# Raw tiles of the second MLP matrix move into room of their own, and the first pair's final norm is due three steps later

## The chip, the cores and the metric

The kernel runs on one core of a Trainium2 chip. The metric is the device time of one execution in microseconds (us), taken as the median of several runs; lower is better. Profiled executions show where the time goes. The engines are TensorE (PE, with its weight loads as PEld), VectorE (DVE), ScalarE (ACT), GpSimd (POOL) and SyncE (SP), which does nothing here but issue transfers.

## The reference

One decoder layer on 2048 positions of width 1024, all in float32, and a final norm:

```python
h = rms_norm(x, norm1_g)
proj = einsum('bsd,dc->bsc', h, w_in)             # u_a, v_a, val_b, gate_b, 512 columns each
a_out = gelu(u_a) * (tril(w_s) @ layer_norm(gelu(v_a)) + b)      # in chunks of 128 positions
b_out = silu(group_layer_norm(conv31(val_b * sigmoid(gate_b))))  # causal, depthwise
x = x + einsum('bsc,cd->bsd', concat([a_out, b_out]), w_out)
h = rms_norm(x, norm2_g)
x = x + einsum('bsf,fd->bsd', relu(h @ w_ff1) ** 2, w_ff2)       # 1024 -> 4096 -> 1024
return rms_norm(x, final_g)
```

## The kernel before, in words

**Tiles.** The positions are four blocks (b = 0..3) of 512. Activations lie with features on the 128 partitions and positions along the free axis. Every product is done three times in a rounded float32 form, high by high, high by low and low by high (`mm3`, line 177), so each operand exists as a high part (a cast on ScalarE) and a low part (a subtraction, `rest`, line 161, on GpSimd or VectorE).

**Stages.** Input projections, gating and the depthwise convolution run block by block; the convolution is a chain of 31 VectorE operations over a tile `g` of gated values (`conv_chain`, line 263) with a tail of transposes and a norm (`conv_tail`). The lists `waiting`, `chains` and `tails` hold convolutions not begun, under way, and at their tails. `stage_o` is the output projection of one block. Then the MLP runs for pairs of blocks, pair 0 being blocks 0 and 1. Both MLP products are done by a seven-product scheme on 2 by 2 blocks: i = 1, 5, 6, 2, 7, 3, 4, where products 5, 6, 7, 3 (and on one side others) use sums or differences of blocks.

The order is: `stage_o(0)` and the rest of the front, `stage_o(1)`, the first up projection (`multiply("u0", ...)`), `stage_o(2)`, `stage_o(3)`, the second up projection (`multiply("u1", ...)`), then the down projection, eight pieces of pair 0 and eight of pair 1 (`down_chunk`, line 1175). One product of an up projection is 12 matmuls of 512 columns; an up projection has 112 of them, 16 units of 7. A piece of the down projection has 28 steps of 6 matmuls, in the order of `STEPS`, line 1073.

**The second matrix ahead of time.** `w_2` is prepared while the up projections run: its 16 matrices go through a pipe, `w2st` (line 901), of five stages: load the raw blocks, make the sum or difference, cast the high part, subtract the low part, store the operand to memory. The down projection reads the operands back. How fast the pipe goes is `pace["w2"]`, in steps per call of `beside`: `W2_PACE` has 0.3 in the first up projection, 0.2 in `stage_o(2)`, 0.65 in the second up projection, 0.7 in the down projection. One matrix is seven steps. The pipe's call is `w2st.run(k - 1, k, k + 1, k + 1, k + 2)`: stores up to k - 1, low parts up to k, high parts and sums up to k + 1, loads up to k + 2. The first matrix has a pipe of its own, `wst`, of the same kind. Both are filled by `left` (line 826): `loader` takes two tiles for a matrix, the first with the blocks `r11` and `r12`, the second with `r21` and `r22`, and issues two loads of 512 KB on SyncE; `maker` makes the sums. In the order 1, 5, 6, 2, 7, 3, 4 the first tile is last read when the difference of i = 3 (sixth) is made, the second by the low part of i = 4 (seventh). The last two tiles of each matrix are thus in use for most of its seven steps.

**Room.** `slots` is a pool of 41 tiles of 4 KB a partition. It serves raw tiles, operands, the 28 `hop` tiles (7 sums for each of 4 feature pairs) that an up projection reads, the residual, the down projection's inputs and operands. `gpool` has 7 tiles of 542 floats for `g`. `t2` and `wsum` hold smaller working tiles. A new tile takes a place whose last user is done; an instruction that writes it waits for that user. All queues are in order: a load that waits on SyncE holds up every later one there.

**Order.** Blocks under `tc.manual_schedule()` run in the order in which the code issues them: `stage_o(1)` to the end of the second up projection, and the very last piece. The other pieces of the down projection are ordered by a planner, by the code's order and by what it reckons to be ready.

**The final norm.** When the last sums of a block are added up in the last piece of its pair, `finish(b, acc)` (line 1118) is put into `queue`. Its squares are summed by GpSimd in `square_add`. `tick(n)` advances the first generator of the queue n times. In the down projection a step with j = 3 gives two advances, j = 0 and j = 2 one each, j = 1 none. `finish` lets `gaps[0]` advances pass, sums the squares over the features with narrow matmuls (`ssum`), then makes the reciprocal root, spreads it (`rbc`), and scales and stores eight tiles, one an advance. Block 1's `finish` starts at step (3, 3) of pair 0's last piece; block 0's follows it in the queue.

Of the kernel before, what the change touches and what calls it, by code (L numbers as in the profile page):

```python
# [9 lines left out]
F32 = mybir.dt.float32  # L10
# [5 lines left out]
P = 128  # L16
# [16 lines left out]
G_SLOTS = 7  # L33
T_SLOTS = 10
W_SUMS = 6
# [5 lines left out]
TAIL_STEPS = (3, 1, 2)  # L41
# [41 lines left out]
def hybrid_block_kernel(  # L83
# [26 lines left out]
    def pool(stack, name, bufs, psum=False):  # L110
        return stack.enter_context(tc.tile_pool(
            name=name, bufs=bufs, reuse_waits="tile",
            space=bass.MemoryType.PSUM if psum else bass.MemoryType.SB))

    slots = pool(ctx, "slots", SLOTS)
    gpool = pool(ctx, "gpool", G_SLOTS)
    t2 = pool(ctx, "t2", T_SLOTS)
    wsum = pool(ctx, "wsum", W_SUMS)
    banks = {}
    early = ctx.enter_context(ExitStack())  # L120
    banks["mm"] = pool(early, "ps_mm", MM_BANKS, True)
    banks["cv"] = pool(early, "ps_cv", 2, True)
# [8 lines left out]
    def slot(name, dtype=F32):  # L131
        return slots.tile([P, 1024], dtype, tag="s", name=name)
# [5 lines left out]
    def tmp(name, dtype=F32):  # L138
        return t2.tile([P, 512], dtype, tag="tmp", name=name)
# [4 lines left out]
    def mm_tile(name):  # L144
        return bank("mm", name)
# [4 lines left out]
    def tiny(name, n=4):  # L150
        return small.tile([P, n], F32, tag=f"{name}{n}", name=name)
# [92 lines left out]
    def v(off, j):  # L244
        return vec[:, off + j:off + j + 1]
# [15 lines left out]
    waiting, chains, tails = [], [], []  # L261
# [222 lines left out]
    def feature_sums(acc, n, pc=None):  # L484

        pc = tp_tile("ssum") if pc is None else pc
        for i in range(n):
            for k, sq in enumerate(acc):
                pe4.matmul(pc[:, i:i + 1], sq[:, i * P:(i + 1) * P], ones[:, 0:1],
                           start=k == 0, stop=k == len(acc) - 1)  # L490
        return pc[:, :n]
# [251 lines left out]
    late, _ = stage_v(1, h[1], parts[1])  # L743
# [4 lines left out]
    late, _ = stage_v(2, h[2], parts[2])  # L748
# [9 lines left out]
    late, _ = stage_v(3, h[3], parts[3])  # L758
# [64 lines left out]
    def order_of(units):  # L823
        return ORDER if len(units) == 1 else ORDER2

    def left(src, units, tag):

        raw, sums = {}, {}

        def loader(m):  # L830
            def load():
                raw[m] = [slot("wraw"), slot("wraw")]
                for a in range(2):
                    nc.sync.dma_start(raw[m][a], src[m, a])
            return load

        def maker(m, i):
            def make():
                (r11, r12), (r21, r22) = [(t[:, :512], t[:, 512:]) for t in raw[m]]
                if i in (5, 6):  # L840
                    sums[m, i] = wsum.tile([P, 512], F32, tag="ws", name="ws")
                out, x, y, op = {
                    5: (sums.get((m, 5)), r21, r22, ALU.add),
                    6: (sums.get((m, 6)), sums.get((m, 5)), r11, ALU.subtract),
                    7: (r21, *((r11, r21) if tag == "w2" else (r21, r11)), ALU.subtract),
                    3: (sums.get((m, 5)), r12, sums.get((m, 6)), ALU.subtract)}.get(i, [None] * 4)
                if out is None:
                    return {1: r11, 2: r12, 4: r22}[i]
                dsb.tensor_tensor(out, x, y, op=op)
                return out  # L850
            return make

        for i in order_of(units):
            for m in units:
                yield (tag, m, i), loader(m) if i == 1 else lambda: None, maker(m, i)
# [21 lines left out]
    def multiply(tag, groups, pair, out, at):  # L877
        bks, rhs, n = {}, hops[pair], 0
        for units in groups:
            for i in order_of(units):  # L880
                for m in units:
                    w = wst.get((tag, m, i))
                    out(m, i, product(i, m, bks, w, rhs[i]))
                    used[0] += 1
                    u = used[0]
                    lag = (3, 4, 5, 7) if n > 16 else (2, 3, 4, 6)
                    beat()
                    wst.run(u, *(min(u + k, 112 * (pair + 1)) for k in lag))
                    beside()
                    at(n)  # L890
                    n += 1
# [77 lines left out]
    def up_out(pair):  # L969
        kept = {}  # L970

        def out(m, i, ps):
            blk_ = INTO[i]
            def copy():
                kept[m, blk_] = tmp("c")
                nc.scalar.copy(kept[m, blk_], ps)

            def finish():
                if i == 4:
                    src, c = ps, tmp("c")  # L980
                else:
                    c = kept.pop((m, blk_))
                    src = c if i == 7 else ps
                    dve.tensor_tensor(src, ps, c, op=ALU.add)
                (dsb if i == 7 else dve).scalar_tensor_tensor(
                    c, src, 0.0, r_rows[:, blk_[1], :], op0=ALU.max, op1=ALU.mult)
                later(1, lambda: nc.scalar.activation(c, c, AF.Square))  # L987
                later(2, lambda: nc.scalar.dma_start(
                    f_d[pair][m // 2, 2 * blk_[0] + blk_[1], :, m % 2, :], c))

            later(1, copy if i in (1, 5, 6) else finish, True)
        return out

    def reopen_banks(old, phase, **count):
        old.close()
        st = ctx.enter_context(ExitStack())
        for kind, n in count.items():
            banks[kind] = pool(st, f"ps_{kind}_{phase}", n, True)
        return st
# [52 lines left out]
    with tc.manual_schedule():  # L1052
        stage_o(1, first_at(0))
        multiply("u0", UNITS, 0, up_out(0), at_up0)
    mid = early if waiting or chains or tails else reopen_banks(early, "m", mm=6, tp=2)
    with tc.manual_schedule():
        stage_o(2, at_o2)
        pace["w2"] = 0.0
# [58 lines left out]

    def finish(b, acc):

        gaps = (3, 3, 4) if b < 2 else TAIL_STEPS  # L1120
        for _ in range(gaps[0]):
            yield
        r = tiny("r1")
        ve = tiny("ve")
        ps = feature_sums(acc, 4, mm_tile("ssum"))
        yield
        dve.tensor_scalar(ve, ps, 1.0 / D, EPS, op0=ALU.mult, op1=ALU.add)
        gps.tensor_tensor(r, ve, nhalf.to_broadcast([P, 4]), op=ALU.pow)
        for _ in range(gaps[1]):
            yield  # L1130
        dg = tmp("dg")
        times_ident(dg, r)
        for _ in range(gaps[2]):
            yield
        ps = mm_tile("rbc3")
        pe4.matmul(ps, ones, dg, start=True, stop=True)
        x = dn["x"][b]
        for k in range(KD):
            yield
            dve.scalar_tensor_tensor(x[k], x[k], v(V_FG, k), ps, op0=ALU.mult, op1=ALU.mult)  # L1140
            nc.sync.dma_start(out[b, k // 2, :, k % 2, :], x[k])

    def times_ident(dg, r):
        dsb.tensor_tensor(
            dg.rearrange("p (n t) -> p n t", t=P), ident.unsqueeze(1).to_broadcast([P, 4, P]),
            r.unsqueeze(2).to_broadcast([P, 4, P]), op=ALU.mult)
# [28 lines left out]
    def down_chunk(pair, n, after):  # L1175
# [4 lines left out]
        for i, j in STEPS:  # L1180
            bank_, first = BANK[i]
            a, t = INTO[i]
            if first:
                bks[bank_, j] = mm_tile("py")
            ps = bks[bank_, j]
            for m in range(2):
                hl = [o[:, m * 512:m * 512 + 512] for o in ops[i]]
                mm3(ps, [w2[i][m][:, k, j * P:(j + 1) * P] for k in range(2)], hl,
                    first and m == 0, m == 1)
            x = dn["x"][2 * pair + t][2 * j + a]  # L1190
            dve.tensor_tensor(x, ps, x, op=ALU.add)
            if n == 7 and LAST[a, t] == i:
                done[t] += 1
                last = pair == 1 and t == 0
                square_add(accs[t], x, last and done[t] > 6)
                if done[t] == 8:
                    f = (finish_last if last else finish)(2 * pair + t, accs[t])
                    (ends if last else queue).append(f)
            if j == 3:
                after(n, i)  # L1200
                beside(2)
            elif j == 1:
                beside(0)
            else:
                tick(1)
# [88 lines left out]
```

## Time and profile before

| what | us |
|---|---|
| median of 3 runs | 1842.84 |
| lowest and highest run | 1842.77, 1843.34 |
| the profiled execution | 1846.86 |
| its span, first to last instruction | 1845.0 |

In the span the stages lie as follows, by TensorE's work in the timeline: input projections, gating and output projections of blocks 0 and 1 up to about 491 us, first up projection to 802 us, output projections of blocks 2 and 3 to 892 us, second up projection to 1198 us, down projection to 1830 us. The lines of the profile on which the argument rests stand in the prediction. In a line of groups or of the timeline, "[2.30 <-POOL sq L78]" means that the engine was idle for 2.30 us before this instruction and that an instruction of GpSimd writing a tile `sq` ended that. L78 is the line of a helper through which most operations are issued, so the tile's name tells more than the line.

### The profile page before, as it was taken

Reading aid. Unit: us, or ns where it says so; the run is one execution under the profiler, and the core shown is the slowest. Engines: PE = TensorE matmul, PEld = TensorE weight load, DVE = VectorE, ACT = ScalarE, POOL = GpSimd, SP = SyncE. Lnnn points to the kernel's source line nnn. Section 1 sums busy time; section 2 is a strip of 40 time slices with the busy share of each in tenths; the row PEclk is TensorE's granted clock in tenths of the full one; section 3 lists DMA queues with packets and bytes.
Section 4 is the critical chain, followed back from the end, with each engine's and each line's share of the span. In section 5 each row is a group of like instructions: output and inputs, shape, how many; then the busy total and the mean of one; then the engine's idle time right before and its main releaser. Section 6 shows DMA issues by size and latency. Waiting matters only on the chain.

```text
span 1845.0 us, 23225 instructions
## 1 busy us (share of the span) xinstructions
PE 1810.2 (98%) x8068; PEld 1492.0 (81%) x8068; DVE 1340.5 (73%) x1826; ACT 757.7 (41%) x1169; POOL 1232.4 (67%) x774
## 2 busy tenths in 40 slices
PE   9999989999999999999999999999999999999996
PEld 7888877888888888888887887888788878888885
DVE  5699997997899985632566686778766668665555
ACT  5345554554445455455454545433312131222112
POOL 4575984983766667699777988777855465444434
PEclk9999999999999999999999999999999999999998
DMA  8342654532545455685556878999987779767742
GB/s 323 112 165 93 222 177 180 204 131 82 209 151 196 162 193 201 216 294 197 205 187 227 294 251 292 355 399 375 374 336 259 256 248 333 294 240 259 263 162 91
DMA packets 131685, 424.72 MB, mean 230 GB/s; under 512 B 14576, under 2 KB 15216, under 8 KB 131568
## 3 DMA queue, kind: packets, MB, share of 16 engines
q1 hardware_dynamic: 96288, 329.64, 50.5%
q10 hardware_dynamic: 35280, 93.60, 13.0%
q8 instruction: 63, 1.03, 0.2%
q14 instruction: 54, 0.44, 0.1%
HBM read 302.60 MB, written 120.59 MB: 229 GB/s over the span
## 4 chain that ended last, share of the span: by engine, by line
PE 85%; DVE 7%; POOL 3%; DMA 2%; issue 2%; ACT 1%; SPq 0%; DVEq 0%; ACTq 0%; POOLq 0%
PE py L78 48%; PE pz L78 8%; PE po L78 8%; PE px L78 4%; PE pg L78 4%; PE pvv L78 4%; PE pu L78 4%; DVE acc L78 3%; PE pv L78 3%; DMA wraw<-in_w 1%; PE sgu L78 1%; DVE nb L78 1%; DVE ws L78 1%; PE rbc L78 1%; POOL sq L78 1%
## 5 line engine op out<-in xcount | busy, mean ns | idle before, releaser
L78 PE MATMUL py<-fo_hi,w2o 128*128 128x512 f32 x1792 | 555.6, 391 | 0.0
L78 POOL TENSOR_TENSOR fo_lo<-fraw,fo_hi 128x1024 fp32r<-128x1024 f32 x111 | 275.6, 2493 | 255.4 <-ACT fo_hi L158 219.9
L78 DVE TENSOR_TENSOR x<-py,x 128x512 f32<-128x512 f32 x448 | 299.8, 687 | 181.1 <-PE py L78 180.9
L78 PEld LDWEIGHTS py<-fo_hi,w2o 128*128 128x128 f32 x1792 | 337.3, 188 | 70.5 <-issue 0.5
L78 PE MATMUL py<-hop,w1o 128*128 128x512 f32 x1536 | 364.2, 391 | 4.0 <-ACT w1o L806 2.3
L78 PE MATMUL py<-fo_lo,w2o 128*128 128x512 f32 x896 | 350.1, 391 | 1.5 <-POOL fo_lo L78 1.4
L78 PEld LDWEIGHTS py<-hop,w1o 128*128 128x128 f32 x1536 | 287.5, 188 | 66.5 <-ACT w1o L806 3.1
L78 DVE SCALAR_TENSOR_TENSOR acc<-g,vec,acc 128x512 f32<-128x512 f32 x464 | 322.8, 746 | 1.2
L158 ACT CAST fo_hi<-fraw 128x1024 fp32r<-128x1024 f32 x112 | 116.9, 1052 | 408.2 <-PE py L78 218.6
L78 POOL TENSOR_TENSOR w_lo<-raw,w_hi 128x1024 fp32r<-128x1024 f32 (+1 forms) x94 | 224.2, 2392 | 56.0 <-ACT w_hi L158 39.0
L78 POOL TENSOR_TENSOR w1o<-wraw,w1o 128x512 fp32r<-128x512 f32 x120 | 172.0, 1437 | 58.6 <-ACT w1o L806 48.7
L78 PEld LDWEIGHTS py<-fo_lo,w2o 128*128 128x128 f32 x896 | 168.5, 188 | 38.6 <-POOL fo_lo L78 3.0
L78 PE MATMUL pz<-hop,w1o 128*128 128x512 f32 x768 | 183.8, 390 | 0.0
L78 POOL TENSOR_TENSOR w1o<-ws,w1o 128x512 fp32r<-128x512 f32 x90 | 128.7, 1433 | 67.4 <-ACT w1o L806 66.1
L78 PEld LDWEIGHTS pz<-hop,w1o 128*128 128x128 f32 x768 | 143.8, 188 | 29.7
L78 DVE TENSOR_TENSOR fraw<-fraw 128x1024 f32<-128x1024 f32 x64 | 94.9, 1483 | 13.9 <-POOL fo_lo L78 13.8
L78 PE MATMUL po<-m_hi,w_hi 128*128 128x512 f32 x256 | 101.2, 395 | 0.0
L78 PE MATMUL po<-m_hi,w_lo 128*128 128x512 f32 x256 | 99.9, 390 | 0.6 <-POOL w_lo L78 0.6
L987 ACT ACTIVATE c<-c 128x512 f32<-128x512 f32 x128 | 80.7, 631 | 48.0 <-DVE c L78 46.6
L78 PE MATMUL po<-m_lo,w_hi 128*128 128x512 f32 x256 | 99.7, 389 | 0.0
L78 POOL TENSOR_TENSOR w2p<-wraw,w2p 128x512 fp32r<-128x512 f32 x64 | 93.7, 1465 | 3.8 <-ACT w2p L806 3.8
L78 DVE TENSOR_TENSOR px<-px,c 128x512 f32<-128x512 f32 x32 | 22.4, 699 | 101.0 <-PE px L78 69.9
(150 smaller groups left out, 2956.7 us busy)
## 6 DMA issues: line engine op xcount, KB each, us to landing
w2o<-w_d SPq DMA_DIRECT2D x224, 512.0 KB, 6.2
w_d<-w2p ACTq DMA_DIRECT2D x112, 512.0 KB, 5.1
wraw<-in_w SPq DMA_DIRECT2D x92, 512.0 KB, 4.9
f_d<-c ACTq DMA_DIRECT2D x128, 256.0 KB, 4.1
fraw<-f_d SPq DMA_DIRECT2D x64, 512.0 KB, 6.9
raw<-in_w_ct SPq DMA_DIRECT2D x48, 512.0 KB, 5.2
raw<-in_w_o SPq DMA_DIRECT2D x32, 512.0 KB, 5.1
w1o<-w_d SPq DMA_DIRECT2D x28, 512.0 KB, 5.7
```

The lines of the kernel that those rows point to most:

```text
L78: return op(out, *args, **kwargs)
L158: nc.scalar.copy(hi, src)
L987: later(1, lambda: nc.scalar.activation(c, c, AF.Square))
```

## The change

The pool `gpool` is opened last among the working pools, in a stack of its own. When the first up projection is issued, `gpool` is closed and a pool of three 4 KB tiles, `more["w2"]`, is opened in its place. From then on the loader of `w_2` takes its two raw tiles from there instead of from `slots`; the loader of `w_1` has no entry in `more` and goes on with `slots`. The PSUM banks are reopened at that point without the condition that stood there. In `finish`, the first gap for blocks 0 and 1 is 6 advances instead of 3.

```diff
     slots = pool(ctx, "slots", SLOTS)
-    gpool = pool(ctx, "gpool", G_SLOTS)
-    t2 = pool(ctx, "t2", T_SLOTS)
-    wsum = pool(ctx, "wsum", W_SUMS)
-    banks = {}
+    sb = ctx.enter_context(ExitStack())
+    t2 = pool(sb, "t2", T_SLOTS)
+    wsum = pool(sb, "wsum", W_SUMS)
+    gst = sb.enter_context(ExitStack())
+    gpool = pool(gst, "gpool", G_SLOTS)
+    banks, more = {}, {}
...
             def load():
-                raw[m] = [slot("wraw"), slot("wraw")]
+                p = more.get(tag)
+                raw[m] = [slot("wraw") if p is None else p.tile(
+                    [P, 1024], F32, tag="m", name="wraw") for _ in range(2)]
                 for a in range(2):
                     nc.sync.dma_start(raw[m][a], src[m, a])
...
         multiply("u0", UNITS, 0, up_out(0), at_up0)
-    mid = early if waiting or chains or tails else reopen_banks(early, "m", mm=6, tp=2)
+    mid = reopen_banks(early, "m", mm=6, tp=2)
+    gst.close()
+    more["w2"] = pool(sb, "more", 3)
     with tc.manual_schedule():
         stage_o(2, at_o2)
...
-        gaps = (3, 3, 4) if b < 2 else TAIL_STEPS
+        gaps = (6, 3, 4) if b < 2 else TAIL_STEPS
         for _ in range(gaps[0]):
             yield
```

## The prediction, made before the change was run

> **What bounds the kernel now.** I read the page first, then the waits of TensorE from the last product of the first pass onward, then the stages as windows, then the waits of SyncE's queue, and last the timeline around each TensorE stop.
>
> ```profile
> span 1845.0 us, 23225 instructions
> PE 1810.2 (98%) x8068; PEld 1492.0 (81%) x8068; DVE 1340.5 (73%) x1826; ACT 757.7 (41%) x1169; POOL 1232.4 (67%) x774
> ```
>
> TensorE is busy 98% of the span, so 34.8 us is all that any change to waits could win, and most of that lies where this change cannot reach. The waits of TensorE from 800 us to 1560 us (who <- whom: us in total, times, longest) are what it can reach:
>
> ```profile
> PE py L78 <- ACT w1o L806: 2.3, 1, 2.3
> PE ssum L78 <- POOL sq L78: 2.3, 1, 2.3
> PE py L78 <- POOL fo_lo L78: 1.4, 2, 1.2
> PE py L78 <- ACT c L976: 1.4, 1, 1.4
> PE po L78 <- POOL w_lo L78: 0.6, 1, 0.6
> ```
>
> They sum to 8.0 us. The stages (us, then busy time and count for PE, PEld, DVE, ACT, POOL, then clock, DMA share, GB/s):
>
> ```profile
> 892.00:998.00 106.00, 106.00 (x470) 87.14 (x470) 69.27 (x73) 53.97 (x98) 78.11 (x56) 1.00 0.58 207
> 1109.00:1120.00 11.00, 9.62 (x42) 7.64 (x42) 4.15 (x6) 6.14 (x12) 7.63 (x6) 1.00 0.95 323
> 1180.00:1279.00 99.00, 99.00 (x439) 81.98 (x438) 78.64 (x88) 32.97 (x47) 71.67 (x38) 1.00 1.02 399
> ```
>
> Undisturbed, TensorE does 470 matmuls in 106 us, 0.226 us each. In the second up projection the DMA engines have room (0.58); from 1180 us they are full (1.02). Behind the first and fourth wait stands SyncE. Its own waits in the second up projection, 892 to 1170 us:
>
> ```profile
> SPq L834 <- PE py L78: 82.0, 13, 23.9
> SPq L834 <- DMA w_d<-w2p: 57.2, 12, 8.6
> SPq L834 <- DVE ws L78: 52.5, 6, 17.7
> SPq L834 <- POOL w1o L78: 25.1, 6, 7.6
> ```
>
> Line 834 loads raw weights, `w_1` and `w_2` alike. A load reads an input that nobody writes; what it waits for is a tile of `slots`: the product, the store, the difference or the remainder named is the last user of that tile. So SyncE stands at this line for most of the stage because the 41 tiles are all taken. They hold 28 `hop` tiles (7 sums by 4); 13 are left for raw tiles of two matrices, operands, and operands on their way to memory.
>
> **The change part by part.** First the room.
>
> ```profile
> L78 DVE SCALAR_TENSOR_TENSOR c<-g,vec,acc x16: 731/738/748, 114.5 to 682.1; 128x512 f32<-128x512 f32 x16
> L309 ACT ACTIVATE y<-cb,vec x8: 760/774/790, 420.0 to 711.0; 128x512 f32<-128x512 f32 x8
> ```
>
> The last tap reads a `g` tile at 682.1 us and the last tail ends by 712 us; the reopening stands behind the first up projection, whose last products run until 802 us. So the three lists in the condition on line 1055 are empty, the unconditional reopening does what was done before, and opening the new pool waits for nothing. The room suffices: seven tiles of 542 floats are 15,176 bytes a partition, three of 1024 floats are 12,288. No instruction is added or removed.
>
> What moves is which tile a `w_2` load gets. One matrix holds two raw tiles for seven steps; at 0.65 steps a product that is 10.8 products, 29 us, and the next pair is loaded before the first is free. So two to four of the 13 loose tiles come back to `w_1`, operands and stores. What that is worth is read at the two stops:
>
> ```profile
> 990.59 8.85 SPq L834 DMA_DIRECT2D wraw<-in_w  x4
> 996.90 1.73 POOL L78 TENSOR_TENSOR w2p<-wraw,w2p 128x512 fp32r<-128x512 f32 x1
> 1004.82 0.62 ACT L806 CAST w1o<-wraw 128x512 fp32r<-128x512 f32 x1 [4.01 <-DMA wraw<-in_w]
> 1007.42 0.62 ACT L806 CAST w1o<-ws 128x512 fp32r<-128x512 f32 x1 [1.45 <-DVE ws L78]
> 1008.08 2.08 PE L78 MATMUL py<-hop,w1o 128*128 128x512 f32 x8 [2.31 <-ACT w1o L806]
> ```
>
> Four loads take SyncE 8.85 us, where four issues of 0.33 us would take 1.3: the second pair stood until the remainder of a `w2p`, ending at 998.63 us, gave up its raw tile. That pair is `w_1`'s (its cast makes a `w1o`); it landed 4 us after ScalarE wanted it, and TensorE stopped 2.31 us. Issued some 7 us earlier it is in time: **-2.3 us**.
>
> ```profile
> 1107.47 1.37 DVE L78 TENSOR_TENSOR ws<-wraw,ws 128x512 f32<-128x512 f32 x1
> 1108.99 3.68 SPq L834 DMA_DIRECT2D wraw<-in_w  x4
> 1117.38 0.62 ACT L806 CAST w2p<-wraw 128x512 fp32r<-128x512 f32 x1 [3.74 <-POOL w1o L78]
> 1117.91 0.58 ACT L976 COPY c<-py 128x512 f32<-128x512 f32 x1
> 1118.54 3.02 PE L78 MATMUL py<-hop,w1o 128*128 128x512 f32 x12 [1.38 <-ACT c L976]
> ```
>
> Here two pairs leave together right after a difference freed a tile. ScalarE then stands 3.74 us before a cast of a raw `w_2` tile (the releaser named had ended before; I take it to be the load), the copy queued behind it clears the bank late, and TensorE stops 1.38 us. A first tile free beforehand lets the load go ahead: **-1.4 us**. Both bounds of these two terms: 0 if something else is late at once, -3.7 as taken. Below that nothing is to be had there, since no other stop stands in the stage.
>
> What is late next is what the three tiles cost. Pair m takes tiles A and B, pair m+1 C and A, so the second load of a pair waits until step 3 of the matrix before has made its difference (sixth of seven steps), one step (1.5 products, about 4.2 us) before the load's own place. Behind that wait stand all later loads on SyncE, `w_1`'s among them. The first operand needs tile C only, and tile A is first read three steps, some 12 us, after it came free. A load takes
>
> ```profile
> wraw<-in_w SPq DMA_DIRECT2D x42, 512.0 KB, 5.1
> w2o<-w_d SPq DMA_DIRECT2D x70, 512.0 KB, 8.7
> ```
>
> 5.1 us here (second row: 8.7 us for the operands' reloads once the engines are full, 1180 to 1360 us), so the cover is about 7 us, and I cost this wait at 0; without cover it is a rival below.
>
> The down projection has one stop of this kind, at its third piece:
>
> ```profile
> 1303.55 0.50 PE L78 MATMUL py<-fo_lo,w2o 128*128 128x512 f32 x1 [1.20 <-POOL fo_lo L78]
> 1170.60 3.03 SPq L1068 DMA_DIRECT2D x<-x_d  x3
> ```
>
> Transfers are full from 1180 us, so what starts earlier before then is a lead that lasts. The residual's eight reloads begin at 1170.60 us, behind the last waiting raw loads, while the engines have room; two or three tiles more start two or three of them earlier, at 1.3 us each (0.5 MB at 399 GB/s) a lead of 2.6 to 3.9 us against stops of 1.4 in sum. I take **-1.4 us**; its bounds are -1.4 and, if the order of the loads turns out worse, the same stop doubled, +1.4. The 0.6 us at `w_lo` stays: GpSimd runs
>
> ```profile
> 844.56 7.11 POOL L78 TENSOR_TENSOR w_lo<-raw,w_hi 128x1024 fp32r<-128x1024 f32 x3
> ```
>
> three in a row there, and no raw `w_2` tile is in its way.
>
> Now the norm three steps later. `finish(1)` is queued at step (3,3) of the pair's last piece; with a gap of 3 its sums come due after (2,2), step 23 of 28, with 6 after (4,0), step 25. But the stage up to there is ordered by the planner:
>
> ```profile
> 1197.00:1511.20 314.20, 304.48 (x1338) 250.85 (x1338) 1.00 0.86 324
> 1507.51 4.97 POOL L78 TENSOR_TENSOR sq<-sq 128x512 f32<-128x512 f32 x4
> 1511.30 1.05 PE L78 MATMUL ssum<-ones,sq 128*128 128x1 f32 x8 [2.30 <-POOL sq L78]
> 1512.44:1515.85 3.41, 3.41 (x9) 2.63 (x9) 0.81 (x2) 0.87 (x1) 3.34 (x3) 0.50 0.58 204
> 1522.51 5.34 DVE L78 SCALAR_TENSOR_TENSOR x<-x,vec,rbc 128x512 f32<-128x512 f32 x8
> ```
>
> The first row counts the matmuls with a `w2o` before the sums: 1338 = 7 x 168 + 162, so they stand after step 27, not 23. The last row shows why: eight scalings that the code spreads over eight ticks run back to back, so the planner places what it reckons ready. It reckoned the squares ready only at step 27; a due step of 25 is still earlier, and the place stays. The stop costs 2.3 us and then 3.41 us at half clock, where 9 matmuls ran instead of 15: 6 x 0.226 = 1.4. Bounds 0 and **-3.7**; I take 0, because the rule read off the rows gives it. The eight scalings and stores come later by some 3 us for one block and 6 for the other; they end long before the span does and cost nothing.
>
> The half clock follows a stop of 2.3 us plus eight matmuls one column wide, while the 2.31 us stop at 1008 us left the clock at 1.00. The Trainium skill, page "TensorE: Matmul & The Clock Gate", section "Why this matters for your kernels", asks for idle gaps over some 3 us before the rate drops; by it alone the norm's term would be 2.3. The trace has the drop after a shorter one, and decides.
>
> Sum against the profiled execution: -2.3 - 1.4 - 1.4 = **-5.1 us** of 1846.86 us (span 1845.0 us and 1.9 around it). That execution lies 4.0 us over the median of the runs, 1842.84 us; the stops are waits, so I carry the same -5.1 over: 1837.7 us.
>
> **The rivals.** (a) The norm's stop goes as well: the planner's place slips past the end of the piece, or slots shift GpSimd's order. For it: two steps are 12 x 0.226 = 2.7 us, more than the 2.3 missing. Against: the readiness above. -5.1 - 3.7 = -8.8: **1834.0**.
>
> (b) Transfers or ScalarE's order keep the stops: the load is not late for its tile but for the engines. For it: DMA share 0.95 around the second stop. Against: 0.58 before the first. Then only the first goes, -2.3: **1840.5**, or, with a new small stop, no change. The Trainium skill, page "DMA: Bandwidth & Descriptors", section "Issuing engines are not separate DMA queues", says that all transfers share 16 engines and interleave whoever starts them; where they are full an earlier issue buys nothing, as rows of 5.1 and 8.7 us bear out.
>
> (c) Slower: three tiles are too few. If VectorE makes step 3's difference more than 4.2 us behind its place, SyncE stands at the pair's second load and the next `w_1` load leaves late, as at 1004.82 us. About eight `w_2` matrices pass in this stage; each may cost a stop like the two seen, 1.4 to 2.3, so 11 to 18 us against 5.1 won; with half of them hit, +1 to +4, with all, +6 to +13. I take +6: **1849**. It decides from a lag of 4.2 us. For it: the difference at 1107.47 us freed a tile late. Against: VectorE is busy 65% there (69.27 of 106).
>
> **How the numbers follow.** 0.2% is 3.7 us, about what a measurement of this kernel tells from no change. Chances: forecast 0.34, (a) 0.27, (b) 0.25, (c) 0.14. The forecast alone spans 1837 to 1841 (the `w_lo` stop going too gives 1837.1, the third term at +1.4 gives 1840.5). The range goes past (a) to 1831.5 and up to 1847, the mild half of (c), leaving out 0.05 below and 0.1 above. Faster by over 0.2% (below 1839.2): (a) and most of the forecast, 0.59; within 0.2%: (b) and the rest, 0.27; slower: (c), 0.14.
>
> **What would show it.** Right: SyncE's waits at the raw load fall from the 217 us of the four rows to under half; the rows `w1o L806` and `c L976` leave TensorE's waits; the `ssum` row stays at about 2.3 with its stretch of clock 0.50, and 1338 matmuls stand before it. Rival (a): that stretch is gone. Rival (c): SyncE waits at the raw load for `DVE ws`, and `w1o` rows multiply. Wrong altogether: new stops where the planner orders the down projection anew.

## The result and the profile after

| | before | after |
|---|---|---|
| median of 9 runs each, us | 1846.65 | 1836.19 |
| lowest to highest, us | 1842.77 to 1852.39 | 1834.01 to 1843.06 |
| the profiled execution, us | 1846.86 | 1834.01 |
| its span, us | 1845.0 | 1832.2 |

The runs of both kernels were made side by side on one chip. The ratio is 0.995, with a 95% interval of 0.9935 to 0.9965: faster, by 0.35 to 0.65%. The forecast was 1837.7 us, with a range of 1831.5 to 1847.0.

The head of the page of after:

```profile
span 1832.2 us, 23223 instructions
PE 1805.3 (99%) x8068; PEld 1489.0 (81%) x8068; DVE 1328.6 (73%) x1826; ACT 757.8 (41%) x1169; POOL 1234.8 (67%) x774
```

The waits of TensorE from 800 to 1560 us in after (who <- whom: us in total, times, longest):

```profile
PE ssum L78 <- POOL sq L78: 1.0, 1, 1.0
PE py L78 <- POOL fo_lo L78: 0.9, 2, 0.6
PE py L78 <- DVE x L78: 0.7, 1, 0.7
PE po L78 <- POOL w_lo L78: 0.6, 1, 0.6
```

They sum to 3.2 us, from 8.0. Both rows of the second up projection are gone, the row of the sums (`ssum`) fell from 2.3 to 1.0, and the third piece of the down projection has two rows, 1.6 us, where it had one of 1.4. A stop is such idle time of TensorE.

The lengths of the two stages concerned are read from the first and last start of the products that read a `hop` tile (850 to 1250 us), and from the stretch that holds the first eight pieces' 1344 matmuls with a `w2o` (its row: start and end, length, then busy time and count of TensorE and of its weight loads, then clock, DMA share and GB/s). Before:

```profile
L78 PE MATMUL py<-hop,w1o x768: 386/389/795, 892.0 to 1202.8; 128*128 128x512 f32 x192
```

```profile
1203.00:1514.74 311.74, 306.99 (x1345) 252.62 (x1344) 1.00 0.86 321
```

After:

```profile
L78 PE MATMUL py<-hop,w1o x768: 387/389/793, 884.6 to 1191.0; 128*128 128x512 f32 x192
```

```profile
1191.23:1501.18 309.95, 306.28 (x1344) 251.79 (x1344) 1.00 0.84 323
```

From its first product to that of the next stage, the second up projection went from 311.0 us (892.0 to 1203.0; the 1198 us given for its end in the section on time and profile are 5 us too early) to 306.6 (884.6 to 1191.2), and pair 0's pieces from 311.7 to 310.0. Pair 1's pieces became 0.6 us shorter. Together that is -6.7. The two spans differ by 12.8 us. The rest lies ahead of the first up projection, which begins at 491.0 us before and at 484.3 after, where no instruction was changed. Before's profile has one long stop there that after's has not; its waits of TensorE from 200 to 300 us begin

```profile
PE ct L78 <- ACT c L300: 4.5, 1, 4.5
```

and 6.83 us at half clock follow. Of the kernels below, the one that changes only the gap, and so has before's own front, ended it at 484.4 us, and the one that changes only the layout at 483.5, while one with the whole room took 489.3 and has that stop again (3.8 us). So these 6.7 us are the luck of one execution, not the change.

The time at half clock can be taken out by an estimate, the mean time multiplied by the mean granted clock. For after's nine runs it is 1823.7 us (1836.8 x 0.9929). The clock of before's nine runs was not kept; 28 runs of before in the next series give 1830.5 us (1845.2 x 0.9920), 6.8 more. The same estimate within one series, for the changed kernel run again (e13_again), is 1824.7 against 1830.4 us, 5.7 apart. At full clock the change is worth some 6 to 7 us by these, as by the stages.

### The profile page after: what moved, and what is told of

It reads as the page before. It is cut to its first block, busy times and chain, and to the rows that moved or that the text cites. A ratio compares the mean times of both kernels' runs of the same rounds, so it can differ in the third digit from the quotient of the medians.

```text
span 1832.2 us, 23223 instructions
## 1 busy us (share of the span) xinstructions
PE 1805.3 (99%) x8068; PEld 1489.0 (81%) x8068; DVE 1328.6 (73%) x1826; ACT 757.8 (41%) x1169; POOL 1234.8 (67%) x774
## 4 chain that ended last, share of the span: by engine, by line
PE 86%; DVE 4%; DMA 4%; POOL 3%; issue 2%; ACT 1%; SPq 0%; DVEq 0%; POOLq 0%; ACTq 0%
PE py L78 45%; PE pz L78 9%; PE po L78 9%; PE px L78 5%; PE pg L78 4%; PE pv L78 4%; PE pu L78 4%; PE pvv L78 3%; DVE acc L78 2%; POOL fo_lo L78 1%; POOL w2p L78 1%; DMA raw<-in_w_v 1%; DMA w2o<-w_d 1%; DMA w_d<-w2p 1%; PE sgu L78 1%
```

## The experiments

The kernels' parts of the second up projection ("up") and of pair 0's eight pieces ("down"), each from its one profile, read as above; median times and ratios to the kernel before, measured beside each, with 95% intervals. "w_2 tiles" is how many `w_2` has of its own after the first up projection ("first pass"), "gap" the first gap of `finish` in advances of the queue. In the four kernels with a gap of 12 the sums stand behind the eight pieces, so "down" leaves out the sums themselves, some 0.9 us, and any stop at them.

| kernel | w_2 tiles | gap | up | down | median | ratio |
|---|---|---|---|---|---|---|
| before | 0 | 3 | 311.0 | 311.7 | 1846.65 | 1 |
| e3_layout_only | 0 | 3 | 311.1 | 311.9 | 1843.84 | 1.0001 (0.9986 to 1.0016) |
| e2_gap_only | 0 | 6 | 310.2 | 309.3 | 1843.02 | 0.9992 (0.9977 to 1.0008) |
| e1_room_only | 3 | 3 | 306.8 | 312.1 | 1837.61 | 0.9962 (0.9948 to 0.9975) |
| after | 3 | 6 | 306.6 | 310.0 | 1836.19 | 0.9950 (0.9935 to 0.9965) |
| e13_again | 3 | 6 | 307.0 | 309.9 | 1836.83 | 0.9964 (0.9947 to 0.9981) |
| e7_gap12 | 3 | 12 | 306.9 | 307.8 | 1835.45 | 0.9953 (0.9935 to 0.9971) |
| e9_gap0 | 3 | 0 | 306.9 | 322.2 | 1852.33, one run | |
| e6_two_tiles | 2 | 6 | 318.3 | 310.5 | 1847.73 | 1.0025 (1.0009 to 1.0042) |
| e8_slots38_room | 3, and 38 `slots` | 6 | 313.8 | 309.0 | 1849.71 | 1.0031 (1.0018 to 1.0044) |
| e10_pace75 | 3 | 12 | 312.1 | 305.3 | 1835.68 | 0.9963 (0.9948 to 0.9977) |
| e11_pace70 | 3 | 12 | 309.5 | 309.0 | 1840.47 | 0.9972 (0.9956 to 0.9988) |
| e12_pace_first | 3 | 12 | 307.9 | 310.3 | 1839.98 | 0.9979 (0.9964 to 0.9993) |
| e14_down_slots | 3, up only | 6 | 307.0 | 309.3 | 1835.56 | 0.9955 (0.9939 to 0.9971) |

### Which part does it: room, gap, layout

The room with the old gap:

```diff
-        gaps = (6, 3, 4) if b < 2 else TAIL_STEPS
+        gaps = (3, 3, 4) if b < 2 else TAIL_STEPS
```

> The changed kernel with the first gap back at 3. Theory (the room ends the two stops of the second up projection, the gap ends the half clock at the pair's end): the two stops `w1o L806` 2.3 us and `c L976` 1.4 us stay gone, `ssum` waits 2.3 us again behind 1338 matmuls and the half clock of 3.4 us comes back, so 3 to 4 us slower than the changed kernel and 5 to 7 us faster than before (ratio to before 0.996 to 0.997). Rival (the planner orders the pieces anew because of the room): `ssum` stands elsewhere without the gap too, and the time is that of the changed kernel (0.995). Rival (the room's new place in memory speeds the front): see the layout run.

The gap alone, on the kernel before:

```diff
-        gaps = (3, 3, 4) if b < 2 else TAIL_STEPS
+        gaps = (6, 3, 4) if b < 2 else TAIL_STEPS
```

> The kernel before with the first gap at 6 and nothing else. Theory: `ssum` moves from behind 1338 matmuls to behind 1344, waits about 1 us instead of 2.3, and the half clock there goes; the two stops of the second up projection stay at 2.3 and 1.4; 2 to 3.7 us faster than before (ratio 0.998 to 0.999). Rival (the place of `ssum` is set by readiness alone): `ssum` stays behind 1338 matmuls with its 2.3 us and the ratio is 1.000.

The order of the pools, the early end of `gpool` and the unconditional reopening, without the three tiles:

```diff
     gst.close()
-    more["w2"] = pool(sb, "more", 3)
...
-        gaps = (6, 3, 4) if b < 2 else TAIL_STEPS
+        gaps = (3, 3, 4) if b < 2 else TAIL_STEPS
```

> The changed kernel's order of pools, `gpool` opened last and closed after the first up projection, but nothing opened in its place: the second matrix's raw tiles come from `slots`, first gap 3. Theory (the 7.4 us by which the changed kernel's profile reaches 838.6 instead of 846.0 us are chance of the front, which no edit touches): ratio to before 1.000 within 0.002, and stops of 2.3, 1.4 and 2.3 us as before. Rival (the tiles' new addresses speed the front): the front ends some 7 us earlier than before in every profile and the ratio is 0.996.

The waits of TensorE (790 to 1560 us) in the room alone:

```profile
PE py L78 <- DVE x L78: 2.4, 1, 2.4
PE ssum L78 <- POOL sq L78: 2.3, 1, 2.3
```

in the gap alone:

```profile
PE py L78 <- ACT w1o L806: 1.5, 1, 1.5
PE py L78 <- POOL fo_lo L78: 1.4, 2, 1.2
PE py L78 <- ACT c L976: 1.4, 1, 1.4
PE ssum L78 <- POOL sq L78: 1.0, 1, 1.0
```

and in the layout alone:

```profile
PE ssum L78 <- POOL sq L78: 2.3, 1, 2.3
PE py L78 <- ACT w1o L808: 2.2, 1, 2.2
PE py L78 <- POOL fo_lo L78: 1.4, 2, 1.2
PE py L78 <- ACT c L980: 1.3, 1, 1.3
```

The stops at `w1o` and `c` stand in all three kernels without the tiles (before among them; at `w1o` between 1.5 and 2.3 us) and in neither of the two with them; the sums' stop is 2.3 with a gap of 3 and 1.0 with one of 6. The layout alone is the kernel before. In time, the room alone carries the change, a ratio of 0.9962; the gap alone cannot be told from no change by its ratio (0.9992, interval across 1). The estimate at full clock, mean time by mean clock within this one series, sees a little of it: 1830.5 us for before, 1830.5 for the layout, 1828.9 for the gap and 1825.7 for the room, each with a standard error of 0.3 to 0.6 over its runs.

The profiles say that the gap gains: pair 0's pieces took 311.7 to 312.1 us in three kernels with a gap of 3, 309.0 to 310.5 in six with 6. Not all of that is the gap's. Its own part is the stop, 1.3 us shorter. Between before and the gap alone the other 1.1 is the half clock from 1512.44 us, of which 2.3 us, at half rate, fall into these pieces; but the room alone, with the same stop of 2.3 us, has no half clock there, against what was expected of it. It has a longer stop in the third piece instead, the 2.4 us at `x`, where after has 0.7.

### Does the number of tiles count, or that they are apart?

Three tiles of their own, taken out of `slots`:

```diff
-SLOTS = 41
+SLOTS = 38
```

> The changed kernel with 38 tiles in `slots` instead of 41, so that the 3 new tiles and these make 41 together, as before. Theory (what counts is how many tiles are left to the first matrix's loads and the operands): the waits of SyncE at the raw loads come back to about those of before (over 200 us), and stops of 1 to 3 us return in the second up projection; the down projection, which reads ahead with fewer tiles, may add some: time between the changed kernel and before, or above before. Rival (what counts is that long-lived raw tiles are apart from short-lived ones, not the number): no stop in the second up projection, time as the changed kernel, 0.995 to 0.997.

And two tiles instead of three:

```diff
-    more["w2"] = pool(sb, "more", 3)
+    more["w2"] = pool(sb, "more", 2)
```

> The changed kernel with two tiles in the new pool instead of three: a pair's first load then waits for the sixth step's difference of the matrix before, its second for the seventh step's low part, so the cover of the second falls from three steps (12 us) to about one (4 us) against a load of 5 us. Theory (the third tile's cover is what makes the room free of cost): SyncE stands longer at the raw load, casts and sums of raw tiles wait for loads again, stops of 1 to 3 us return in the second up projection and more come in the down projection; time 3 to 12 us above the changed kernel, ratio to before 0.997 to 1.003. Rival (the loads have much more cover than I worked out): time as the changed kernel, 0.995.

With 38 + 3, the same 41 in sum, the up pass took 313.8 us, longer than with 41 shared, and the row of stops at `c` is back, three times:

```profile
PE py L78 <- ACT c L980: 4.7, 3, 2.8
```

The first pass, which has only the 38, went from 310.4 to 319.3 us between its first product and its last. So it does not help by itself that `w_2`'s tiles are apart; what helps is that there are three more. Whether 44 tiles in one pool would do as well was not run. With two tiles the up pass is 11.7 us longer than with three, and so 7.3 longer than before, although there are 43 in sum (the second row lies in the down projection, at 1283 us):

```profile
PE py L78 <- ACT c L980: 4.0, 1, 4.0
PE py L78 <- DMA w2o<-w_d: 3.0, 1, 3.0
PE py L78 <- ACT w1o L808: 2.4, 1, 2.4
```

Its SyncE stands, from 892 to 1170 us, at the raw load for the pool's own tiles eight times, 44.0 us (3.7 in after):

```profile
SPq L838 <- POOL w2p L78: 44.0, 8, 9.7
```

That is rival (c) of the prediction in kind: SyncE stands for the pool's own tiles, and loads behind that come late (the engines stand 24.4 us for raw tiles, 1.1 in after). Not all its signs came: the `w1o` row is there once, 2.4 us, and what SyncE stands longer for is a remainder `w2p`; for VectorE's difference `ws` it stands as long as in after (92.4 and 92.2 us). The stops in the pass, with 0.7 us at a `w2p`, sum to 7.1 us, and two stretches of 3.41 us at half clock stand in it (1001.41 and 1093.58 us). The third tile is what keeps this away.

### Where the sums stand

A gap of 12, and one of 0:

```diff
-        gaps = (6, 3, 4) if b < 2 else TAIL_STEPS
+        gaps = (12, 3, 4) if b < 2 else TAIL_STEPS
```

> The changed kernel with a first gap of 12 instead of 6, so that the sums are due at step 4 of the next piece (step 32), past the place they have now. Theory (the planner puts `ssum` at its due step or when it reckons the squares ready, whichever is later, and that is about step 27 to 28): `ssum` stands behind some 1368 matmuls, GpSimd has long finished, the 1.0 us stop goes, and the time is 0 to 1 us below the changed kernel's, ratio to before 0.994 to 0.996. Rival (the place is always four steps behind the due one): it stands behind 1392 or so, same time. Rival (later stores hold tiles that the down projection wants for reading ahead): new `fo_lo` stops in pieces 8 and 9 and a time 1 us or more above.

> The changed kernel with a first gap of 0: the sums are due right at step (3,3), 20 of 28. Theory (readiness sets the place): `ssum` still stands behind 1338 matmuls and waits about 2.3 us. Rival (a fixed lag of four steps behind the due one): it stands behind 1320 and waits some 6 us for GpSimd, with a half clock after it. Where the place falls in between, neither holds alone.

The matmuls with a `w2o` from the start of the down projection to the first sum, as windows. Gap 0:

```profile
1197.14:1507.08 309.94, 300.89 (x1320) 247.17 (x1319) 0.99 0.84 321
```

Gap 6, the changed kernel:

```profile
1191.23:1500.27 309.04, 306.28 (x1344) 251.76 (x1343) 1.00 0.85 323
```

Gap 12:

```profile
1191.00:1504.29 313.29, 311.66 (x1368) 256.26 (x1367) 1.00 0.85 323
```

At six matmuls a step (7 x 168 = 1176 lie ahead of the last piece), the sums stand after step 24, 28 and 32; with a gap of 3 it is 27. They come due after steps 20, 25 and 32, and 23. (Three advances more, 6 for 3, moved the due step by two, 23 to 25; the "three steps" of the title are advances.) The place follows the due step, with a lag that shrinks from 4 to 0; so neither readiness alone nor a fixed lag holds. With gap 0 the sums stand there before their squares are ready:

```profile
PE ssum L78 <- POOL sq L78: 7.4, 1, 7.4
```

In all three that stop, gaps 0, 3 (308.30 us in the prediction's kernel, 1203.00 to 1511.30) and 6, the sums start 308.3 to 309.9 us after the down projection does, wherever they stand in TensorE's order. GpSimd's squares set that moment. A later place only puts more products ahead of it; at gap 12 enough of them, and the stop is gone. The kernel with 12 is not told from the one with 6 by time (0.9953 and 0.9950).

### The changed kernel again, and other paces

> The changed kernel again, beside the two pace runs on one chip, so that they can be told apart from it. Expected: ratio to before 0.995 within 0.0015, the second up projection 306.6 us long, `ssum` behind 1344 matmuls with a stop of 1.0 us.

The same kernel in a second series: 1836.83 us, the second up projection and pair 0's pieces within 0.4 us (307.0 and 309.9). The sums' stop is 1.0 us as in the first profile, but here 3.41 us at half clock follow it, and pair 1's pieces take 311.4 us from first to last product, for 309.9; on that the last section.

Could the `w_2` pipe now go faster in the second up pass (0.75 and 0.70 for 0.65), or in the first (0.36 for 0.30)? All with a gap of 12:

```diff
-W2_PACE = (0.3, 0.2, 0.65, 0.7)
+W2_PACE = (0.3, 0.2, 0.75, 0.7)
```

> Gap 12 and the second matrix's pace in the second up projection at 0.75 steps a product instead of 0.65, so some 8 steps (8 stores of 512 KB and about 1 pair of loads, 5 MB) leave the stage from 1180 us on, where the transfer engines are full, for the second up projection, where they are not. Theory (the 1.6 us of stops left in the third piece of the down projection come of full transfer engines): these stops go, the second up projection stays at about 306.6 us, time 1 to 3 us below the gap-12 run. Rival (GpSimd, ScalarE or the loads of the second up projection have no room for it): new stops there of 1 to 4 us, time equal or above.

> Gap 12 and a pace of 0.70 in the second up projection. At 0.75 the third piece's stops went (2.5 us won) and stops of 3.7 us came in the second up projection, because a pair of raw tiles is wanted every 9.3 products instead of 10.8. Theory (there is a pace between at which both are small): 1 to 2 us below the gap-12 run, ratio to before 0.994 to 0.995. Rival (the two are exchanged one for one): same time as the gap-12 run, 0.995 to 0.996.

> Gap 12 and the second matrix's pace in the first up projection at 0.36 instead of 0.30, 5 steps earlier; there the raw tiles still come from `slots`. Theory (tiles of `slots` are scarce there too, as the 38-tile run with 8.5 us more in the first up projection says): the third piece's stops shrink by 1 to 1.6 us, but stops of 1 to 4 us come in the first up projection; time equal or above the gap-12 run. Rival (the first up projection has room): 1 to 1.6 us below it.

At 0.75 the third piece's stops all but vanish, and stops come into the up pass:

```profile
PE py L78 <- ACT c L980: 3.7, 3, 1.7
PE py L78 <- POOL fo_lo L78: 0.2, 1, 0.2
```

312.1 + 305.3 us for 306.9 + 307.8: what the down projection wins, the up pass more than pays. The row at `c` has an old name, but no engine waits for a raw load in this stage; before the longest one ScalarE stands 3.29 us in front of a cast of a `w2p`, and the profile names a store to `w_d` as what ended that. At 0.70 the up pass takes 309.5 us and the third piece has stops of 2.2; with the faster first pass one stop of 4.1 us at a `fo_hi` stands in the third piece, where shorter ones were expected. The medians of these two are 3.6 and 3.2 us above that of the changed kernel in the same series, with intervals that overlap. No pace tried beats the changed kernel.

### What holds the third piece

In after, SyncE stands in the down projection for a tile of the new pool. It waits at line 838, the raw load, which takes only such tiles there; why the first row names a store, which uses no raw tile, was not followed. Its waits from 1255 to 1276 us and its timeline:

```profile
SPq L838 <- DMA w_d<-w2p: 8.7, 1, 8.7
SPq L838 <- POOL w2p L78: 4.6, 1, 4.6
```

```profile
1257.92 3.22 SPq L1114 DMA_DIRECT2D w2o<-w_d  x4
1274.43 0.33 SPq L838 DMA_DIRECT2D wraw<-in_w  x1
```

The last run gives the down projection the old tiles back, and keeps the new ones for the up pass:

```diff
     reopen_banks(mid, "d", mm=8)
+    more.clear()
```

(Two slips in the text below: `slots` has 41 tiles, not 34, and it is the second matrix that has the new pool.)

> The changed kernel with the second pool emptied once its last first-matrix tile has been taken, so that all raw loads of the down projection come from the 34 first slots again, as in the kernel before; the first matrix keeps the three tiles, the gap stays at 6. Theory: SyncE's standing at a tile of the second pool (1261.1 to 1274.4 us in the changed kernel's profile, with the transfer engines' share at 0.72 in 1267 to 1290) is what holds the third piece of the down projection; then its stops for fo_lo and x (1.6 us together) go, pair 0's eight pieces take about 308.4 us instead of 310.0, and the time is about 1.5 us below the changed kernel's. Rival 1: the stops come from the chain from GpSimd's fo_lo over VectorE to ScalarE's fo_hi, which the raw loads do not set; then pair 0's pieces stay at 309.7 to 310.3 us with 1 to 2 us of stops for fo_lo, and the time is the changed kernel's within 1 us. Rival 2: the three tiles help the down projection too, since w_2's raw loads no longer wait for a slot; then its first pieces get longer, by 1 us or more, and stops for w2o or w_d appear there. The u pass of pair 1 stays at 306.6 to 307 us under all three.

SyncE's standing at the raw load fell from 13.3 us (the two rows above) to 2.5 between 1250 and 1300 us, and stops stayed, 1.4 us instead of 1.6. So the theory is out, and rival 1 is nearest, by the time and the stops; pair 0's pieces, 309.3 us, lie 0.4 below its range, and the chain is not the one it names. The row of 0.7 at `x` left, and the old row is back:

```profile
PE py L78 <- POOL fo_lo L78: 1.4, 2, 1.2
```

Its place is that of before to a few hundredths: 1292.42 - 1191.87 = 100.55 us into the down projection, 1303.55 - 1203.00 = 100.55 before. What leads to it, in this run, ScalarE and then GpSimd:

```profile
1280.83 6.19 ACTq L903 DMA_DIRECT2D w_d<-w2p  x3
1287.11 0.62 ACT L808 CAST w2p<-wraw 128x512 fp32r<-128x512 f32 x1 [7.53 <-POOL w2p L78]
```

```profile
1282.99 2.41 POOL L78 TENSOR_TENSOR fo_lo<-fraw,fo_hi 128x1024 fp32r<-128x1024 f32 x1
1285.36 1.30 POOL L78 TENSOR_TENSOR w2p<-wraw,w2p 128x512 fp32r<-128x512 f32 x1
1287.81 1.75 POOL L78 TENSOR_TENSOR w2p<-wraw,w2p 128x512 fp32r<-128x512 f32 x1 [1.15 <-ACT w2p L808]
1289.52 5.21 POOL L78 TENSOR_TENSOR fo_lo<-fraw,fo_hi 128x1024 fp32r<-128x1024 f32 x2
```

ScalarE issues the stores of finished operands, in order with its casts. The last of three stores waits for GpSimd's remainder of a `w2p`, which ends at 1286.66 us; ScalarE has stood 7.53 us when the cast behind it starts; GpSimd, which makes the next remainder from that cast, stands 1.15 us; and the `fo_lo` queued behind it is 1.22 us late for TensorE. Before's trace has the same rows (7.54 and 1.15). No load stands in these rows. After's own two stops, 0.65 us at a `fo_lo` and 0.74 at `x`, have no such row ahead of them: ScalarE's longest wait from 1276 to 1292 us is there 4.4 us, for VectorE. What sets them was not followed.

## Why the prediction was right, and where not

**The room, two stops, -3.7.** Right. Both rows left, in every kernel with 41 + 3 tiles and the old paces, and the up pass is 4.2 to 4.4 us shorter (306.6 and 306.8 for 311.0), a little beyond the bound of -3.7: besides the stops, 0.6 us of TensorE's busy time went. That the rows left because there are three tiles more, not because the tiles are apart, is shown by the kernel with 38 + 3. Rival (b), by which the full engines keep the second stop, is out: that stop left as well. (That an earlier issue buys nothing where the engines are full is not shown by any run; the rows of 5.1 and 8.7 us show only how long a load takes to land.)

**Rival (c) at cost 0.** Right for three tiles. Half of its sign came all the same: SyncE's waits for `DVE ws` at the raw load rose from 52.5 to 92.2 us, and TensorE had no stop from it. With two the rival came, and the kernel was slower than before (1.0025).

**The norm's term, taken as 0.** Wrong. The step that failed is "the place stays", read from the eight scalings as a planner that goes by readiness. The gap-0 kernel refutes it: there the sums stand 7.4 us ahead of their squares. The due step moves the place, and three advances moved it by one step, 1338 to 1344 matmuls. That took 1.3 us off the stop, and in some executions the half clock behind it. Pair 0's pieces differ by -2.4 (before and e2) and -2.1 us (e1 and after), inside the bounds 0 and -3.7; of that 1.3 is the gap's in both, the rest is half clock in the one and, in the main, the stop at `x` in the other. The prediction's own signs say the same: `ssum` was to keep its 2.3 us behind 1338 matmuls with the half clock, and the sign of rival (a), that this stretch is gone, is what after's profile shows (its second profile has the half clock again). Rival (a), which let the whole stop go, is half right: it goes at 12, not at 6. Why the place lags the due step by 4, 4, 3 and 0 stays open.

**The third piece, -1.4.** Wrong: 1.4 before, 1.6 after. The step was that an earlier start of the residual's reloads is a lead that lasts. They did start earlier, at

```profile
1157.57 0.88 SPq L1074 DMA_DIRECT2D x<-x_d  x2
1165.29 6.65 SPq L1074 DMA_DIRECT2D x<-x_d  x6
```

but the down projection moved up with them: the first two leave 33.7 us ahead of its start now, 32.4 before, a lead of 1.3 and not 2.6 to 3.9, and the last of the eight 19.3 now, 20.1 before. And it would have bought nothing at this stop, since in before it comes from ScalarE's stores.

**The sum.** -5.1 was forecast; the stages show -6.7, the room's 4.4 with 1.7 and 0.6 in the down projection. The two errors, the norm's term too little and the third piece's too much, partly cancel. That the median lies only 1.5 us below the forecast is chance as well: the forecast stood on a median of before of 1842.84, and beside after before's was 1846.65. Against that one the gain is 10.5 us, 5.4 more than forecast, of which the stages explain 1.6. How the rest divides between less time at half clock and the spread of nine runs over 9 us is not known. In the second series the same two kernels lie 7.5 us apart (1844.29 and 1836.83).

**The marker at SyncE.** Wrong. Its waits at the raw load were to fall from 217 us to under half; from 892 to 1170 us after has

```profile
SPq L838 <- DVE ws L78: 92.2, 9, 21.0
SPq L838 <- PE pz L78: 63.4, 5, 23.7
SPq L838 <- DMA w_d<-w2p: 57.2, 10, 13.8
SPq L838 <- POOL hop L78: 13.3, 2, 7.7
```

226 us, though the pass is 4.4 us shorter. SyncE runs ahead until something holds it; here its waiting time did not measure lateness. What fell is the idle time of the others before a raw tile's first use, in the view of `wraw` for the same stretch. Before:

```profile
  DMA wraw<-in_w: 14.5, 8
```

After:

```profile
  DMA wraw<-in_w: 1.1, 1
```

That row should have been the marker. Without the tiles it is 14.5 to 16.6 us in three kernels, with three tiles beside 41 and the old paces 1.1 us or none, with two tiles 24.4. It tells of late raw loads alone and does not scale with time: with 38 + 3 it is 7.2, less than before, in a longer pass.

## What to carry to other kernels

An in-order load queue in front of a full pool makes one consumer's late release another's late load; a few more tiles are worth the stops that this causes, and one tile fewer than the reuse needs can cost more than they win (11.7 us against 4.4 here). To see whether it is so, read the idle time of those who use the tile, not the waits of the queue that loads it. Where a narrow product waits for a slow engine, its place in the order only decides how much other work goes first, so put it behind the moment at which its inputs are ready in the trace, with a step to spare; here that ended the stop, though the runs cannot tell the last 1.0 us of it in time. And a store issued from an engine's own queue can hold up the work behind it there.

## What the runs showed of the hardware

Whether half clock follows a stop goes by how much idle time falls into one window of a grid, not by the length of the stop alone. The stretches at half clock start on a grid. In before (stretch, then TensorE's busy time and count, and so on; the clock is the third number from the end):

```profile
246.09:249.50 3.41, 3.41 (x14) 3.06 (x15) 3.41 (x6) 3.40 (x5) 0.17 (x1) 0.50 0.83 286
276.81:283.64 6.83, 4.58 (x13) 3.82 (x14) 6.83 (x11) 1.50 (x4) 0.73 (x2) 0.50 0.01 2
```

and the third at 1512.44 in the prediction: 30.72 and 1266.35 us after the first, 9 and 371 times 3.4133 us. In all fourteen profiles every such start up to the last 50 us of the span fits its own grid. The Trainium skill, page "TensorE: Matmul & The Clock Gate", section "Part 1: The HAM clock gate", gives such a window of 3413 ns that runs freely; the trace agrees. Its condition of a whole idle window does not hold here. Take the windows of that grid from 780 to 1800 us in the fourteen profiles, and in each 3.41 us less the time of the matmuls of 512 columns, so that the one-column sums count as idle: of the windows at full clock, all with 1.93 us or more (ten) are followed by half clock, none with 1.86 or less is. The two on either side of the limit are that of the changed kernel's second series,

```profile
1500.76:1504.17 3.41, 2.39 (x16) 1.81 (x15) 1.36 (x3) 2.15 (x3) 3.41 (x3) 1.00 0.82 292
1504.17:1507.58 3.41, 3.41 (x10) 2.63 (x9) 2.36 (x3) 0.00 (x0) 3.41 (x3) 0.50 0.84 312
```

where a stop of 1.0 us and the sums (0.91 us up to the next product) fall into one window, 1.93 us together, and that of the room alone,

```profile
1501.22:1504.64 3.42, 2.47 (x15) 2.21 (x16) 0.16 (x1) 0.00 (x0) 3.42 (x3) 1.00 0.87 293
```

where a stop of 2.3 us is cut by a boundary into 1.37 and 0.95, and the second part and the sums make 1.86. It also answers what the prediction left open: the 2.31 us at 1008 us in before were cut into 1.50 and 0.81, the 2.30 us at the sums fell into one window whole. In these profiles a little over half a window of idle time or narrow work (the limit lies between 1.86 and 1.93 of 3.41 us), if it falls into one, cost 3.41 us or more at half rate; which windows it falls into changes from one execution to the next, as after's two profiles show.
